# A grouped softmax on one ring of six tiles: the inner block and the clean-up taken out, the semaphores given to the context

## Chip, cores, metric

One NeuronCore of a Trainium2 chip. The metric is device time in microseconds (us). All runs told here were fast (none was clearly slower than the others of its kernel, and the granted clock was 1.0 in each). "Span" is the time from the first to the last instruction of a profiled run; the device time is 1.8 us longer than the span (1330.5 to 1328.7).

## What is computed

```python
B, N, D, G = 4, 4096, 4352, 8          # float32
x_g = x.reshape(B, N, G, D // G)       # groups of 544
e = np.exp(x_g - x_g.max(axis=-1, keepdims=True))
out = (e / e.sum(axis=-1, keepdims=True)).reshape(B, N, D)
```

16384 rows of 17 KB are read once and written once: 285.21 MB each way.

## The kernel before

A tile is 256 rows: 128 partitions of two rows (4.25 MB). Six tile buffers form a ring, and a tile is overwritten in place by its exponentials and then by its results. There are 64 tiles. Three engines work: SP (the sync engine) issues loads and stores, the vector engine (DVE) finds the maxima and scales, the scalar engine (ACT) takes exponentials and sums. DVE and ACT run a hardware loop of ten turns of twelve rows, and eight rows after it.

```python
    ctx.enter_context(tc.tile_critical(no_gpsimd_drain=True))
    ctx.enter_context(nc.cleanup_on_exit())              # clears the semaphores at the end, then a barrier
    bufs = [...]                                         # six tiles
    landed = [nc.alloc_semaphore(f"landed{b}") for b in range(NT)]
    stored = [nc.alloc_semaphore(f"stored{b}") for b in range(NT)]
    ...                                                  # max_done, exp_done, rec_done, scaled

    with nc.Block(no_gpsimd_drain=True) as block:        # ends in a barrier of all engines
        @block.sync
        def _(sync):
            def load(t):
                b = t % NT
                if t >= NT:
                    sync.wait_ge(stored[b], 16 * (t // NT))
                sync.dma_start(out=bufs[b][:, :], in_=xt[t]).then_inc(landed[b], 16)

            for t in range(NT - 1):
                load(t)
            for t in range(nt):
                sync.wait_ge(scaled, R * (t + 1))
                sync.dma_start(out=ot[t], in_=bufs[t % NT][:, :]).then_inc(stored[t % NT], 16)
                if t + NT - 1 < nt:
                    load(t + NT - 1)
            for b in range(NT):                          # the last wait for stores
                sync.wait_ge(stored[b], 16 * ((nt - b + NT - 1) // NT))

        @block.vector
        def _(vector):
            vector_max(0)
            with loop(vector):                           # nc.Fori, its head pinned to slot 0
                for s in range(S):
                    vector_max((s + 1) % S)
                    vector_scale(s)
            ...                                          # the last eight rows
        @block.scalar
        def _(scalar):
            ...                                          # the same with scalar_exp
```

Of the kernel before, what the change touches and what calls it, by code (L numbers as in the profile page):

```python
# [1 line left out]

# [5 lines left out]


@with_exitstack  # L10
def kernel(
    ctx: ExitStack,
    tc: tile.TileContext,
    x: bass.AP,
    out: bass.AP,
):
    nc = tc.nc
    G = 8
    P = 128
    R = 2  # L20
    NT = 6
    S = R * NT
    xf = x.flatten_outer_dims()
    of = out.flatten_outer_dims()
    N, D = xf.shape
    Dg = D // G
    nt = N // (P * R)
    nr = nt * R
    turns = (nr - 1) // S
    f32 = mybir.dt.float32  # L30
    X = mybir.AxisListType.X
    Exp = mybir.ActivationFunctionType.Exp
    xt = xf.rearrange("(t p r) d -> t p (r d)", p=P, r=R)
    ot = of.rearrange("(t p r) d -> t p (r d)", p=P, r=R)

    ctx.enter_context(tc.tile_critical(no_gpsimd_drain=True))  # L36
    ctx.enter_context(nc.cleanup_on_exit())
    bufs = [ctx.enter_context(nc.sbuf_tensor(f"xt{b}", [P, R * D], f32)) for b in range(NT)]
    mx = ctx.enter_context(nc.sbuf_tensor("mx", [P, S, G], f32))
    sm = ctx.enter_context(nc.sbuf_tensor("sm", [P, S, G], f32))  # L40
    rs = ctx.enter_context(nc.sbuf_tensor("rs", [P, S, G], f32))
    landed = [nc.alloc_semaphore(f"landed{b}") for b in range(NT)]
    stored = [nc.alloc_semaphore(f"stored{b}") for b in range(NT)]
    max_done = nc.alloc_semaphore("max_done")
    exp_done = nc.alloc_semaphore("exp_done")
    rec_done = nc.alloc_semaphore("rec_done")
    scaled = nc.alloc_semaphore("scaled")

    def row(s):
        b, r = divmod(s, R)  # L50
        return bufs[b][:, r * D:(r + 1) * D].rearrange("p (g d) -> p g d", g=G)

    def vector_max(s):
        if s % R == 0:
            nc.vector.sem_inc(landed[s // R], -16).wait_op(landed[s // R], 16, "sem-ge")  # L55
        nc.vector.reduce_max(out=mx[:, s, :], in_=row(s), axis=X, negate=True).then_inc(max_done, 1)  # L56

    def vector_scale(s):
        nc.vector.sem_inc(exp_done, -1).wait_op(exp_done, 1, "sem-ge")  # L59
        nc.vector.reciprocal(out=rs[:, s, :], in_=sm[:, s, :]).then_inc(rec_done, 1)  # L60
        nc.vector.sem_inc(rec_done, -1).wait_op(rec_done, 1, "sem-ge")  # L61
        xr = row(s)
        for g in range(G):
            i = nc.vector.tensor_scalar_mul(  # L64
                out=xr[:, g, :], in0=xr[:, g, :], scalar1=rs[:, s, g:g + 1])
        i.then_inc(scaled, 1)

    def scalar_exp(s):
        nc.scalar.sem_inc(max_done, -1).wait_op(max_done, 1, "sem-ge")  # L69
        xr = row(s)  # L70
        for g in range(G):
            i = nc.scalar.activation(  # L72
                out=xr[:, g, :],
                in_=xr[:, g, :],
                func=Exp,
                bias=mx[:, s, g:g + 1],
                scale=1.0,
                accum_out=sm[:, s, g:g + 1],
            )
        i.then_inc(exp_done, 1)  # L80

    def loop(engine):

        return nc.Fori(
            0, turns, engines=OrderedEngineSet([engine.engine]), head_slot={engine.engine: 0})

    with nc.Block(no_gpsimd_drain=True) as block:  # L87


        @block.sync  # L90
        def _(sync):
            def load(t):
                b = t % NT
                if t >= NT:
                    sync.wait_ge(stored[b], 16 * (t // NT))
                sync.dma_start(out=bufs[b][:, :], in_=xt[t]).then_inc(landed[b], 16)

            for t in range(NT - 1):
                load(t)
            for t in range(nt):  # L100
                sync.wait_ge(scaled, R * (t + 1))
                sync.dma_start(out=ot[t], in_=bufs[t % NT][:, :]).then_inc(stored[t % NT], 16)
                if t + NT - 1 < nt:
                    load(t + NT - 1)
            for b in range(NT):
                sync.wait_ge(stored[b], 16 * ((nt - b + NT - 1) // NT))


        @block.vector
        def _(vector):  # L110
            vector_max(0)
            with loop(vector):
                for s in range(S):
                    vector_max((s + 1) % S)
                    vector_scale(s)
            for n in range(turns * S, nr):
                if n + 1 < nr:
                    vector_max((n + 1) % S)
                vector_scale(n % S)

        @block.scalar
        def _(scalar):
            scalar.preload_act_table(Exp)  # L123
            with loop(scalar):
                for s in range(S):
                    scalar_exp(s)
            for n in range(turns * S, nr):
                scalar_exp(n % S)


# [1 line left out]
_INS = ['x']  # L132
_OUTS = [((4, 4096, 4352), 'float32')]


# [23 lines left out]
```

## Time and profile before

| | before |
|---|---|
| device time, median of 3 runs | 1330.23 us (1329.97 to 1331.25) |
| share of the data queue in what 16 DMA engines have | 99.6% |
| DVE busy, ACT busy | 1041.5 us (78%), 764.4 us (58%) |
| steady beat, from load to load | 20.57 us per tile |
| from the end of the last wait for stores to the end of the span | 2.3 us |

The lines that carry this stand in the prediction. Read them in this order: is an engine full (no); is the data queue full (yes); does SP wait for arithmetic or for stores (for stores); how long is the beat.

### The profile page before, as it was taken

To read this page: it belongs to the slowest core of one execution; us is meant where nothing else is said; L and a number is where in the kernel's file an instruction comes from. 1 tells how busy PE (TensorE), PEld (TensorE's weight loads), DVE (VectorE), ACT (ScalarE), POOL (GpSimd) and SP (SyncE) were. 2 spreads that over 40 slices of the span, in tenths; PEclk is the share of its full clock that TensorE was granted. 3 is DMA by queue.
4 is the path that set the end of the run, shared out by engine and by line. 5 is a ranking of instruction groups with operands and counts; after the bars stand their busy time and mean duration, and the time that the engine had idled before them with its cause. 6 is when DMAs were issued, how large, how long until landed. Compare 5 with 4: busy or idle time off the path is not lost. (4 is left out here: it accounts for less than half of the span.)

```text
span 1328.7 us, 4036 instructions
## 1 busy us (share of the span) xinstructions
DVE 1041.5 (78%) x1280; ACT 764.4 (58%) x2049; POOL 0.2 (0%) x4
## 2 busy tenths in 40 slices
DVE  5999987787877878778778787787877877878770
ACT  3777765655656556555565565655655556556560
POOL 0000000000000000000000000000000000000000
DMA  9999999999999999999999999999999999999997
GB/s 401 418 434 434 434 430 428 432 436 433 435 433 431 429 436 434 436 435 430 429 436 434 435 435 432 428 435 435 434 436 434 429 431 436 434 435 434 431 430 336
DMA packets 18441, 570.51 MB, mean 429 GB/s; under 512 B 2048, under 2 KB 2048, under 8 KB 2048
## 3 DMA queue, kind: packets, MB, share of 16 engines
q1 hardware_dynamic: 18432, 570.43, 99.6%
q14 instruction: 9, 0.07, 0.0%
HBM read 285.21 MB, written 285.21 MB: 429 GB/s over the span
## 5 line engine op out<-in xcount | busy, mean ns | idle before, releaser
L72 ACT ACTIVATE xt<-xt,mx 128x544 f32<-128x544 f32 x1024 | 751.3, 735 | 528.7 <-ACTq L69 528.7
L56 DVE TENSOR_REDUCE mx<-xt 128x8 f32<-128x4352 f32 x128 | 599.1, 4680 | 234.0 <-DVEq L55 233.1
L64 DVE TENSOR_SCALAR xt<-xt,rs 128x544 f32<-128x544 f32 x1024 | 434.0, 497 | 19.2 <-DVEq L61 0.9
L72 ACT ACTIVATION_READ_ACCUMULATOR xt<-xt,mx 128x1 f32 x1024 | 191.1, 187 | 0.0
L60 DVE RECIPROCAL rs<-sm 128x8 f32<-128x8 f32 x128 | 24.5, 191 | 3.2 <-DVEq L59 3.2
L123 ACT ACT_TABLE_LOAD x1 | 1.3, 1283 | 0.9 <-SPq L36 0.9
L143 POOL MEMSET const-bfloat16-1.0<- 128x1 bf16 x1 | 0.1, 102 | 0.0
L143 POOL MEMSET const-uint8-127<- 128x1 uint8 x1 | 0.1, 102 | 0.0
L143 POOL MEMSET const-float32-0.0<- 128x1 f32 x1 | 0.1, 99 | 0.2 <-issue 0.2
L143 POOL MEMSET const-float32-1.0<- 128x1 f32 x1 | 0.1, 99 | 0.0
## 6 DMA issues: line engine op xcount, KB each, us to landing
xt<-in_x_dram SPq DMA_DIRECT2D x64, 4352.0 KB, 30.8
out_dram<-xt SPq DMA_DIRECT2D x64, 4352.0 KB, 40.7
```

Source lines behind the costliest of these rows:

```text
L56: nc.vector.reduce_max(out=mx[:, s, :], in_=row(s), axis=X, negate=True).then_inc(max_done, 1)
L60: nc.vector.reciprocal(out=rs[:, s, :], in_=sm[:, s, :]).then_inc(rec_done, 1)
L64: i = nc.vector.tensor_scalar_mul(out=xr[:, g, :], in0=xr[:, g, :], scalar1=rs[:, s, g:g + 1])
L72: i = nc.scalar.activation(out=xr[:, g, :], in_=xr[:, g, :], func=Exp, bias=mx[:, s, g:g + 1], scale=1.0, accum_out=sm[:, s, g:g + 1],)
L123: scalar.preload_act_table(Exp)
L143: nc = _bacc.Bacc("TRN2", target_bir_lowering=False, num_devices=1)
```

## The change

The intent is a plainer program: no inner block with a body per engine, and semaphores that the surrounding context owns and clears once, when it closes. Tiles, ring, loops, waits and arithmetic are as they were.

```diff
+    landed = [tc.alloc_semaphore(f"landed{b}") for b in range(NT)]
+    stored = [tc.alloc_semaphore(f"stored{b}") for b in range(NT)]
+    ...
     ctx.enter_context(tc.tile_critical(no_gpsimd_drain=True))
-    ctx.enter_context(nc.cleanup_on_exit())
     bufs = [...]
-    landed = [nc.alloc_semaphore(f"landed{b}") for b in range(NT)]
-    ...
-    with nc.Block(no_gpsimd_drain=True) as block:
-        @block.sync
-        def _(sync):
-            ...
-        @block.vector
-        def _(vector):
-            ...
+    for t in range(NT - 1):
+        load(t)
+    for t in range(nt):
+        store(t)
+        if t + NT - 1 < nt:
+            load(t + NT - 1)
+    for b in range(NT):
+        nc.sync.wait_ge(stored[b], 16 * ((nt - b + NT - 1) // NT))
+
+    nc.scalar.preload_act_table(Exp)
+    with loop(nc.scalar):
+        ...
+    vector_max(0)
+    with loop(nc.vector):
+        ...
```

More of the change, by code (lines that the diff above doesn't have):

```diff
@@ L34 @@
     ot = of.rearrange("(t p r) d -> t p (r d)", p=P, r=R)
+    landed = [tc.alloc_semaphore(f"landed{b}") for b in range(NT)]
+    stored = [tc.alloc_semaphore(f"stored{b}") for b in range(NT)]
+    max_done = tc.alloc_semaphore("max_done")
+    exp_done = tc.alloc_semaphore("exp_done")
+    rec_done = tc.alloc_semaphore("rec_done")
+    scaled = tc.alloc_semaphore("scaled")
     ctx.enter_context(tc.tile_critical(no_gpsimd_drain=True))
-    ctx.enter_context(nc.cleanup_on_exit())
     bufs = [ctx.enter_context(nc.sbuf_tensor(f"xt{b}", [P, R * D], f32)) for b in range(NT)]
@@ L41, with loop @@
     rs = ctx.enter_context(nc.sbuf_tensor("rs", [P, S, G], f32))
-    landed = [nc.alloc_semaphore(f"landed{b}") for b in range(NT)]
-    stored = [nc.alloc_semaphore(f"stored{b}") for b in range(NT)]
-    max_done = nc.alloc_semaphore("max_done")
-    exp_done = nc.alloc_semaphore("exp_done")
-    rec_done = nc.alloc_semaphore("rec_done")
-    scaled = nc.alloc_semaphore("scaled")
+    def loop(engine):
+        return nc.Fori(
+            0, turns, engines=OrderedEngineSet([engine.engine]), head_slot={engine.engine: 0})
     def row(s):
@@ L80, in scalar_exp @@
         i.then_inc(exp_done, 1)
-    def loop(engine):
-        return nc.Fori(
-            0, turns, engines=OrderedEngineSet([engine.engine]), head_slot={engine.engine: 0})
-    with nc.Block(no_gpsimd_drain=True) as block:
-        @block.sync
-        def _(sync):
-            def load(t):
-                b = t % NT
-                if t >= NT:
-                    sync.wait_ge(stored[b], 16 * (t // NT))
-                sync.dma_start(out=bufs[b][:, :], in_=xt[t]).then_inc(landed[b], 16)
-            for t in range(NT - 1):
-                load(t)
-            for t in range(nt):
-                sync.wait_ge(scaled, R * (t + 1))
-                sync.dma_start(out=ot[t], in_=bufs[t % NT][:, :]).then_inc(stored[t % NT], 16)
-                if t + NT - 1 < nt:
-                    load(t + NT - 1)
-            for b in range(NT):
-                sync.wait_ge(stored[b], 16 * ((nt - b + NT - 1) // NT))
-        @block.vector
-        def _(vector):
-            vector_max(0)
-            with loop(vector):
-                for s in range(S):
-                    vector_max((s + 1) % S)
-                    vector_scale(s)
-            for n in range(turns * S, nr):
-                if n + 1 < nr:
-                    vector_max((n + 1) % S)
-                vector_scale(n % S)
-        @block.scalar
-        def _(scalar):
-            scalar.preload_act_table(Exp)
-            with loop(scalar):
-                for s in range(S):
-                    scalar_exp(s)
-            for n in range(turns * S, nr):
-                scalar_exp(n % S)
@@ new lines, in load, with store @@
+    def load(t):
+        b = t % NT
+        if t >= NT:
+            nc.sync.wait_ge(stored[b], 16 * (t // NT))
+        nc.sync.dma_start(out=bufs[b][:, :], in_=xt[t]).then_inc(landed[b], 16)
+    def store(t):
+        nc.sync.wait_ge(scaled, R * (t + 1))
+        nc.sync.dma_start(out=ot[t], in_=bufs[t % NT][:, :]).then_inc(stored[t % NT], 16)
+    for t in range(NT - 1):
[4 more added lines that the diff above has]
+            load(t + NT - 1)
@@ new lines @@
+    for b in range(NT):
+        nc.sync.wait_ge(stored[b], 16 * ((nt - b + NT - 1) // NT))
+    nc.scalar.preload_act_table(Exp)
+    with loop(nc.scalar):
+        for s in range(S):
+            scalar_exp(s)
+    for n in range(turns * S, nr):
+        scalar_exp(n % S)
+    vector_max(0)
+    with loop(nc.vector):
+        for s in range(S):
+            vector_max((s + 1) % S)
+            vector_scale(s)
+    for n in range(turns * S, nr):
+        if n + 1 < nr:
+            vector_max((n + 1) % S)
+        vector_scale(n % S)
```

## The prediction

The sum came to -1.0 us: -0.5 for the block's exit, -0.5 for the clean-up, +0.1 for the larger clear, -0.1 at the front. The 0.005 for "faster by over 2%": what the trace before shows is that 64 beats of 20.57 us make 1316.5 us, more than the 1303.6 us needed. Rival B: its time of 1329 to 1330 is a guess of mine. So are the 1 to 2 us of rival D. The steps of the block's exit that the trace shows are a branch of SP (38 ns, at 1326.5 us), drains of ACT, DVE and SP, and semaphore steps of all five engines, the last at 1326.7 to 1326.9 us.

> **What bounds the kernel now.** I read the page's busy table and queue table first, then the stretches of the span, the waits of the sync queue, the issues in order of time, and last the instructions of the source lines that the change touches. The first question is whether any engine or only the transfers fill the span:
>
> ```profile
> DVE 1041.5 (78%) x1280; ACT 764.4 (58%) x2049; POOL 0.2 (0%) x4
> DMA  9999999999999999999999999999999999999997
> DMA packets 18441, 570.51 MB, mean 429 GB/s; under 512 B 2048, under 2 KB 2048, under 8 KB 2048
> q1 hardware_dynamic: 18432, 570.43, 99.6%
> q14 instruction: 9, 0.07, 0.0%
> ```
>
> No compute engine is full: the vector engine works 78% of the span. The data queue has packets under way for 99.6% of what 16 DMA engines have in 1328.7 us. All bytes are necessary (285.21 MB in, 285.21 MB out), so the transfers set the time. By stretches (columns: the stretch, its length, busy time and instructions of DVE, ACT, POOL, clock, DMA share, GB/s) the middle is flat:
>
> ```profile
> 35.00:300.00 265.00, 234.16 (x288) 171.92 (x462) 0.00 (x0) 1.00 1.00 431
> 600.00:900.00 300.00, 239.69 (x299) 175.67 (x471) 0.00 (x0) 1.00 1.00 434
> 1290.00:1329.00 39.00, 5.14 (x13) 3.99 (x12) 0.00 (x0) 1.00 0.80 345
> ```
>
> Only the last 39 us fall off (345 GB/s), and there compute has almost ended. Who waits for whom confirms it. The sync queue waits for transfers, not for arithmetic:
>
> ```profile
> SPq L96 <- DMA out_dram<-xt: 1141.2, 58, 20.7
> SPq L102 <- DVE xt L64: 102.4, 6, 33.3
> SPq L106 <- DMA out_dram<-xt: 28.0, 1, 28.0
> ```
>
> 1141.2 of 1328.7 us are spent before a load, until an old store has landed and freed its buffer. The issues in order of time show the beat:
>
> ```profile
> 1223.44 0.33 SPq L96 DMA_DIRECT2D xt<-in_x_dram  x1
> 1223.81 0.43 SPq L102 DMA_DIRECT2D out_dram<-xt  x1
> 1244.03 0.33 SPq L96 DMA_DIRECT2D xt<-in_x_dram  x1
> ```
>
> A load every 20.59 us. The same view has a load at 956.07 us and the one at 1244.03 us fourteen tiles later, so (1244.03 - 956.07) / 14 = 20.57 us per tile. One tile is 2 x 4352 KB = 8.913 MB, hence 433 GB/s. Per tile the vector engine needs 1041.5 / 64 = 16.3 us and the scalar engine 764.4 / 64 = 11.9 us, so even the vector engine has 4.3 us of slack per tile. 64 x 20.57 = 1316.5 us; the other 12.2 us are start, end and fixed instructions.
>
> [...] only 9 instruction packets (0.07 MB) in the whole span, too few for one reload in each of 10 turns.
>
> **The change part by part.** The title words (six tiles, 256 rows, hardware loops) describe both kernels. The diff leaves tile size, ring depth, order of loads and stores, every wait count, every vector and scalar instruction and both loops as they are. Three things change.
>
> (1) The inner block goes. On entry it costs at most a jump per engine. On exit each engine branches, drains and meets the others.
>
> (2) The clean-up on exit goes: a clear of a range of semaphores on POOL and one more barrier of all engines.
>
> (3) The semaphores are now the context's, cleared when it closes. The old trace already has a clear there, so this becomes a larger or a second clear in the same place.
>
> The cost is read from the instructions of each source line (L106 the last wait for stores, L87 the block, _compat.py:109 the clean-up, L154 the context):
>
> ```profile
> L106 SPq EVENT_SEMAPHORE  x3: 17/28/28, 1326.3 to 1326.4; - x3
> L87 SPq COMPARE_BRANCH  x1: 38/38/38, 1326.5 to 1326.5; - x1
> L87 PEldq EVENT_SEMAPHORE  x2: 51/51/51, 1.1 to 1326.9; - x2
> _compat.py:109 POOLq DRAIN  x2: 34/58/83, 1326.9 to 1327.1; - x2
> _compat.py:109 POOLq EVENT_SEMAPHORE_RANGE_CLEAR  x1: 117/117/117, 1327.0 to 1327.0; - x1
> _compat.py:109 PEldq EVENT_SEMAPHORE  x1: 51/51/51, 1327.4 to 1327.4; - x1
> L154 POOLq EVENT_SEMAPHORE_RANGE_CLEAR  x1: 67/67/67, 1328.4 to 1328.4; - x1
> ```
>
> (The two times after the durations are the first and the last start.) The last wait ends at 1326.4, the block's exit runs from 1326.5 to 1326.9, the clean-up from 1326.9 to 1327.4; then the critical section's exit (to 1327.7) and the context's two barriers (to 1328.7) remain. This is a serial chain after the last byte, so all of it lies on the path: 0.5 us for the block's exit and 0.5 us for the clean-up, together 1.0 us. Added: the larger clear. The old clean-up's clear took 117 ns, the context's 67 ns; if it becomes a second instruction, 0.1 us comes back. At the front, the first load starts at 0.95 us and the branches of all engines at 0.8 us (33 ns on SP); if the entry jump goes, the load starts up to 0.1 us earlier, and every transfer with it. Sum: -0.5 - 0.5 + 0.1 - 0.1 = -1.0 us. Between the two ends nothing moves. 1330.23 - 1.0 = 1329.2 us.
>
> **The rivals.**
>
> A: the context needs something the diff does not show, such as a clear or a barrier ahead of the critical section, because its semaphores are taken outside it. A round of barrier plus clear measures 0.5 us (the clean-up), so one such round at the front makes -0.5 us, 1329.7; two cancel the gain, 1330.2. Against it: nothing in the kernel asks for it.
>
> B: the loops are laid out otherwise without blocks of their own, [...] so each turn reloads. [...] Against it: the head is pinned in both kernels. Even then the vector engine has 6 x 4.3 = 26 us of slack per turn of six tiles (an estimate from the two rates above), so a stall of some us per turn vanishes under the transfers[...]. Time: 1329 to 1330.
>
> C: the first tiles run otherwise and the DMA queue runs dry at the start. The first store is issued at 37.5 us; the fifth load, issued by 3.7 us, needs 54.5 us to land, so it lands at about 58. The queue has some 20 us of work in hand; a few tenths cannot empty it. No change.
>
> D: the ragged end moves. The last store is issued at 1297.9 and waited for 28.0 us. The DMA share falls to 0.54 in 1318 to 1322, 0.28 in 1322 to 1324 and 0.08 in 1324 to 1326: some of the 16 engines finish us before the others. Which one is last may differ by 1 to 2 us[...]. That has no direction, and is the main cause of the width of my range.
>
> E: the vector engine becomes the bound. It would need over 4.3 us more per tile; no instruction is added to it. I give it nothing.
>
> **Range and chances.** The three runs before lie in 1329.97 to 1331.25, so chance alone is about +-0.6 us. The sum has an error of about 0.5 us (A, the clears), the ragged end about 1 us. I predict 1329.2 us, 1327.9 to 1330.8 in 8 of 10. 2% is 26.6 us. Faster by over 2% would need 1303.6 us[...]: 0.005, for an error in my reading. Slower by over 2% needs a stall of 26 us that reaches the transfers, which the slack in B and C absorbs: 0.01. Within 2%: 0.985.
>
> **What would show each step right or wrong.** Right: same busy times of DVE and ACT within 1 us, the same packets and MB, loads still 20.57 us apart, the last wait for stores ending near 1326.4, then only about 1.3 us to the end of the span where there were 2.3, no lines of the block and no clean-up clear, and a somewhat longer or second clear at L154's successor. Rival A shows as barriers ahead of the first load, which then starts after 1.2 us instead of 0.95. B shows as over 20 instruction packets and gaps on DVE and ACT once per turn. D shows as a last landing that has moved by more than 1 us with an unchanged chain behind it. The prediction is wrong if the load interval leaves 20.57 us in the middle of the span, or if the instructions behind the last landing take 2 us or more.

## The result

The first comparison had four runs of each kernel: 1330.57 us after (1330.07 to 1331.24) and 1330.49 us before (1329.97 to 1331.25). The ratio is 1.0, with a 95% interval of 0.9983 to 1.0018. (A ratio here is the mean time of one kernel's fast runs over that of the other's of the same rounds, so not quite the ratio of the medians quoted.) The time lies in the predicted range, but the microsecond that I had expected to gain is not to be seen in it.

The page of the changed kernel, the same parts as before:

```profile
DVE 1041.5 (78%) x1280; ACT 764.4 (57%) x2049; POOL 0.2 (0%) x4
...
q1 hardware_dynamic: 18432, 570.43, 99.5%
q14 instruction: 8, 0.07, 0.0%
```

Busy times and data packets are the same. The packed traces have eight instruction packets of 8 KB at much the same moments in both kernels (at 2, 7, 18, 24, 80, 110, 755 and 1243 us before), so the loops do not fetch their code anew in each of their ten turns. The ninth packet of before starts 0.1 us before the end of its span; it comes up again below. The waits of the sync queue (engine, line, waited for: us in total, times, longest):

```profile
SPq L92 <- DMA out_dram<-xt: 1141.8, 58, 21.3
SPq L96 <- DVE xt L69: 102.0, 6, 33.3
SPq L105 <- DMA out_dram<-xt: 28.0, 1, 28.0
```

These are the three waits of before to 0.6 us. Then the closing instructions by source line (L105 is the last wait for stores, L43 the critical section, L149 the context; the last two times are the first and the last start):

```profile
L105 SPq EVENT_SEMAPHORE  x3: 17/28/28, 1328.0 to 1328.1; - x3
...
L43 SPq NOP  x2: 13/13/13, 0.7 to 1328.6; - x2
...
L149 POOLq EVENT_SEMAPHORE_RANGE_CLEAR  x1: 139/139/139, 1329.0 to 1329.0; - x1
```

The block's exit and the clean-up are gone. From the end of the last wait to the end of the last instruction the changed kernel takes 1.28 us, the kernel before 2.29 us: 1.0 us less, the forecast. (These closing times, here and below, are read from the starts and durations in the packed traces, which are kept to the nanosecond; the span that `prof` prints is rounded to 0.1 us.) But the last wait ends 1.7 us later, at 1328.15 instead of 1326.42. Where does that come from? The issues of the sync queue in order of time, before:

```profile
89.19 0.33 SPq L96 DMA_DIRECT2D xt<-in_x_dram  x1
...
109.76 0.33 SPq L96 DMA_DIRECT2D xt<-in_x_dram  x1
...
131.30 0.33 SPq L96 DMA_DIRECT2D xt<-in_x_dram  x1
```

and after:

```profile
89.22 0.33 SPq L92 DMA_DIRECT2D xt<-in_x_dram  x1
...
111.30 0.33 SPq L92 DMA_DIRECT2D xt<-in_x_dram  x1
...
131.84 0.33 SPq L92 DMA_DIRECT2D xt<-in_x_dram  x1
...
1245.77 0.33 SPq L92 DMA_DIRECT2D xt<-in_x_dram  x1
```

At 89 us the two traces are level. The next beat takes 20.57 us before and 22.08 us after, but the one after that 21.54 and 20.54, so at 131 us the changed kernel is only 0.5 us behind. The rest gathers in small steps: 1.5 us at 421 us, 1.6 at 545, 1.7 from 771 us on. The last load is issued at 1244.03 before and 1245.77 after, and in both the last wait ends 82.4 us after it. So the 1.7 us were lost in many beats, most of them in the first third of the run, and not at the end. Either the change makes those beats worse, or they scatter from run to run whatever the kernel. The experiments decide this.

### The profile page after: what moved, and what is told of

Read it like the earlier page. It is cut to its first block, busy times and chain, and to the rows that moved or that the text cites. A ratio compares the mean times of both kernels' runs of the same rounds, so it can differ in the third digit from the quotient of the medians.

```text
span 1329.4 us, 4004 instructions
## 1 busy us (share of the span) xinstructions
DVE 1041.5 (78%) x1280; ACT 764.4 (57%) x2049; POOL 0.2 (0%) x4
## 3 DMA queue, kind: packets, MB, share of 16 engines
q1 hardware_dynamic: 18432, 570.43, 99.5%
## 5 line engine op out<-in xcount | busy, mean ns | idle before, releaser
L77 ACT ACTIVATE xt<-xt,mx 128x544 f32<-128x544 f32 x1024 | 751.2, 734 | 530.4 <-ACTq L74 530.4
```

What stands on the lines that cost most here:

```text
L77: i = nc.scalar.activation(out=xr[:, g, :], in_=xr[:, g, :], func=Exp, bias=mx[:, s, g:g + 1], scale=1.0, accum_out=sm[:, s, g:g + 1],)
```

## The experiments

Theory T1: the change is worth about 1 us in every run, all of it behind the last byte, and the early beats scatter by more than that in both kernels. Rival T2: without the block the transfers themselves run worse and eat the gain. Kernels of one call share the runs of the kernel before on their chip.

### The changed kernel again, and the kernel before as a control

No edit in either; five rounds.

> The changed kernel once more. Theory T1 (the removed closing steps are worth about 1.2 us in every run, and the moment at which the last store lands scatters by 1 to 2 us from run to run, whatever the kernel): the profile shows 1.0 to 1.2 us from the end of the last wait for stores to the end of the span, the last wait ends anywhere in 1325.5 to 1328.5 us, and the median over the rounds is 0.3 to 1.5 us below the kernel before. Rival T2 (without the block the transfers themselves run worse by about 1 to 2 us and eat the gain): the last wait again ends at 1328 us or later, and the two medians are equal within 0.3 us.

> The kernel before, unchanged, as a control. Both theories: a ratio of 1.000 within 0.001. T1: its last wait for stores need not end at 1326.4 us again, it may be off by 1 us or more, and 2.3 us follow it. T2: the last wait ends within 0.5 us of 1326.4.

The last waits, first of the changed kernel again, then of the control:

```profile
L105 SPq EVENT_SEMAPHORE  x3: 17/28/28, 1326.5 to 1326.6; - x3
```

```profile
L106 SPq EVENT_SEMAPHORE  x3: 17/28/28, 1326.5 to 1326.7; - x3
```

The changed kernel's last wait ends at 1326.6 this time, 1.5 us earlier than in its first profile and level with the control's 1326.7. T2 asked for 1328 or later. From there to the end it is 1.28 us in the changed kernel and 2.29 us in the control, as in the first two profiles; for the changed kernel I had expected 1.0 to 1.2, having read the first profile's wait too late. The medians are 1329.84 us (1329.26 to 1329.93) for the changed kernel, 1330.76 us for the control and 1331.42 us for the shared nine runs of before. That is 0.9 us under the control and 1.6 us under the nine, the latter just more than the 1.5 I had allowed. The ratio, 0.9988 (0.9975 to 1.0002), still includes 1. On the control, T1 and T2 differed only in whether its last wait may move: it moved by 0.3 us, which decides nothing.

### Transfers without arithmetic

```diff
     def vector_max(s):
         if s % R == 0:
             nc.vector.sem_inc(landed[s // R], -16).wait_op(landed[s // R], 16, "sem-ge")
-        nc.vector.reduce_max(...)
     def vector_scale(s):
-        ...                        # wait, reciprocal, eight scalings; and all of scalar_exp
+        nc.vector.sem_inc(scaled, 1)
```

> The changed kernel with all arithmetic taken out: the vector engine only waits for a landed tile and counts it as scaled, so loads and stores go on alone (wrong result on purpose). If the transfers set the time, as the prediction says: 1318 to 1332 us, loads 20.5 to 20.7 us apart in the middle. If arithmetic is part of the beat: below 1304 us (faster by over 2%).

Measured: 1330.67 us (1330.09 to 1331.19; result wrong), ratio 0.9994 (0.9979 to 1.0009). Two loads from the middle:

```profile
566.63 0.33 SPq L69 DMA_DIRECT2D xt<-in_x_dram  x1
...
587.22 0.33 SPq L69 DMA_DIRECT2D xt<-in_x_dram  x1
```

Without one maximum, exponential or product the kernel takes as long. The transfers set the time. It also shows the early scatter: its first 18 steady beats (from the seventh load on) together were 4.1 us longer than 18 x 20.57 us, and its last load went out at 1245.71 us, as late as in the first profile of the changed kernel. So neither arithmetic nor its order against the transfers is needed for late beats.

### More work for the vector engine

```diff
+        nc.vector.reduce_max(out=spare[:, s, :], in_=row(s)[:, 0:3, :], axis=X)
         nc.vector.reduce_max(out=mx[:, s, :], in_=row(s), axis=X, negate=True).then_inc(max_done, 1)
```

> The changed kernel with one more reduction over three of eight groups per row (about 1.8 us each, an estimate from 4.68 us for eight groups, so 3.5 us per tile and 227 us in all), results unused. The vector engine then needs 19.8 of 20.57 us per tile. If its slack is off the path, as the prediction says: the time stays within 3 us of the kernel before, the loads still 20.5 to 20.7 us apart. If the vector engine takes part in setting the beat: slower by 20 us or more.

```profile
DVE 1262.3 (95%) x1408; ACT 764.6 (58%) x2049; POOL 0.2 (0%) x4
```

Measured: 1330.62 us (1330.12 to 1332.18), ratio 0.9997 (0.9982 to 1.0012). 220.8 us of added vector work cost nothing: DVE is at 95% and the beat is still 20.57 us. Of the slack of 4.3 us per tile that the prediction leaned on, 220.8 / 64 = 3.45 us were used here without a cost.

### The three steps of the change on twelve tiles

```diff
-    nt = N // (P * R)
+    nt = 12
```

With 12 of 64 tiles there is less run for scatter (less only in part: the uneven beats lie in the first twenty tiles). The middle kernel keeps the block, and takes the semaphores from the context without a clean-up.

> The kernel before on 12 of 64 tiles only (wrong result on purpose: the rest of the output is not written), so that less can scatter between start and end. About 12 x 20.57 + 12 = 259 us. Its closing steps after the last wait should be the 2.3 us of the full kernel.

> The short kernel with the block kept and the clean-up taken out (semaphores of the context): one half of the change. T1: 0.4 to 0.7 us below the short kernel before, and closing steps of 1.6 to 1.9 us. T2 says nothing of this one.

> The changed kernel on 12 of 64 tiles. T1: 1.0 to 1.3 us below the short kernel before, closing steps of 1.0 to 1.2 us, first load at the same 0.95 us. T2: no more than 0.5 us below it, because the transfers end later.

The last waits and the clears of the three, each in its own fence, in this order:

```profile
L106 SPq EVENT_SEMAPHORE  x3: 17/28/28, 236.8 to 257.3; - x3
...
L154 POOLq EVENT_SEMAPHORE_RANGE_CLEAR  x1: 67/67/67, 259.0 to 259.0; - x1
```

```profile
L106 SPq EVENT_SEMAPHORE  x3: 17/27/28, 236.0 to 256.5; - x3
...
L154 POOLq EVENT_SEMAPHORE_RANGE_CLEAR  x1: 157/157/157, 257.7 to 257.7; - x1
```

```profile
L105 SPq EVENT_SEMAPHORE  x3: 17/28/28, 236.4 to 256.9; - x3
...
L149 POOLq EVENT_SEMAPHORE_RANGE_CLEAR  x1: 139/139/139, 257.8 to 257.8; - x1
```

| short kernel | median us | range | last wait to end of span |
|---|---|---|---|
| before | 260.30 | 259.93 to 261.11 | 2.02 |
| block kept, no clean-up | 259.88 | 259.76 to 259.96 | 1.63 |
| changed | 259.35 | 258.98 to 259.98 | 1.27 |

The time falls by 0.42 us with the clean-up and by 0.53 us with the block, 0.95 us together (0.99 by the means). That is slightly less than the 1.0 to 1.3 I had expected, and more than the 0.5 that T2 allowed. But four runs of one kernel spread by up to 1.2 us, and the profiled run of the middle kernel (259.96 us) was no longer than that of the changed one (259.98), so the times do not show the split. The closing steps do: they fall by 0.39 us with the clean-up and by 0.36 us with the block, 0.75 us together. The 1.27 us of the changed kernel lie above the 1.0 to 1.2 I had expected. The fourth combination, clean-up without block, was left out, because in the code nothing would order its clear behind the transfers' increments. The clear of the context grows from 67 to 139 or 157 ns once it takes over the sixteen semaphores.

The short kernel before closes in 2.02 us, and not in the 2.3 of the full one, which I had not expected. The difference is one drain of the vector engine at the closing of the context. The line of the full kernel before, then that of the short one:

```profile
L154 DVEq DRAIN  x2: 10/69/128, 1327.9 to 1328.3; - x2
```

```profile
L154 DVEq DRAIN  x2: 10/10/10, 258.4 to 259.0; - x2
```

In the full kernel before, one of the two drains took 128 ns and started only at 1327.9 us, when ACT, PE and SP had done theirs between 1327.5 and 1327.8. It held up the barrier, whose semaphore steps start at 1328.2 us. The control has it too (130 ns), the changed kernel never (10 ns each in its three profiles). The packed traces show what it goes with: in both, an instruction packet of 8 KB starts 0.67 us after the start of the late drain (at 1328.61 and 1328.87 us). This is the ninth packet of before. The short kernels have no such packet at the end, and in the full changed kernel the next one starts over 1 us after the end of the span. A third late drain, of 144 ns, lies among the twenty blocks at the end below, and a packet follows it after 0.67 us too. So the late drain goes together with an instruction packet that happens to fall into the closing of the kernel before. That the packet is code of the vector engine and holds up its drain is my guess: the trace does not say which engine a packet is for, and no experiment moved it.

### Twenty empty blocks, behind and in front

```diff
+    for _ in range(20):
+        with nc.Block(no_gpsimd_drain=True):
+            pass
```

> The changed kernel with twenty empty blocks behind the last wait for stores. If an empty block at the end lies wholly on the path at the 0.4 to 0.5 us that the old trace shows for the block's exit: 8 to 11 us slower than the changed kernel. If what was seen in the old trace overlapped with waiting anyway: under 3 us.

> The changed kernel with twenty empty blocks ahead of the first load. If the front is as serial as the end: the first load starts about 0.48 us x 20 = 9.6 us later than 0.95 us (0.48 us each is what the twenty at the end gave), and the whole kernel is 8 to 11 us slower; the 20 us of queued work behind the first loads cannot hide what comes before the first byte. If the start is hidden by something: under 3 us.

With the blocks behind the last wait: 1338.99 us (1338.46 to 1339.31), 8.1 us over the kernel before of the same rounds (1330.90), so about 9.1 us over the changed kernel if its gain of 1.0 is counted. The blocks' instructions show the length:

```profile
L126 SPq DRAIN  x20: 7/7/7, 1326.4 to 1335.3; - x20
```

From the first to the twentieth drain 8.9 us pass, so a block costs 8.9 / 19 = 0.47 us on the mean. Most of the 19 steps take 0.44 us; two take 0.86 and 0.72 us, the longer one with the late vector drain. With the blocks in front: 1339.47 us (1339.28 to 1340.03), 9.4 us over the changed kernel of the same rounds (1330.05). Its first load:

```profile
9.79 3.23 SPq L92 DMA_DIRECT2D xt<-in_x_dram  x5
```

The first load starts at 9.79 instead of 0.95 us: 8.84 / 20 = 0.44 us per block. Both ends of this kernel, which is bound by its transfers, are bare: nothing hides a barrier before the first byte or behind the last one. An empty block added costs 0.44 us at either end; taking out the real one gave 0.36 us.

### The loop heads elsewhere

```diff
-            0, turns, engines=..., head_slot={engine.engine: 0})
+            0, turns, engines=..., head_slot={engine.engine: 100})
```

> The changed kernel with the heads of both loops pinned to slot 100 instead of 0[...]. Prediction's rival B: the instruction packets grow from 8 or 9 to 20 or more if reloading happens in each turn, the scalar engine shows a gap once per turn, and the time stays within 2 us all the same, since the vector engine has about 26 us of slack per turn. Against it: slower by 10 us or more.

```profile
q14 instruction: 6, 0.05, 0.0%
```

Measured: 1330.55 us (1330.25 to 1330.62), ratio 0.9996 (0.998 to 1.0011). The packets fell to 6, and ACT's idle time is 529.8 us, as in the other kernels (528.7 before, 530.4 after). The experiment did not bring about the reload that it was to test, so it says only that a shifted loop costs nothing measurable here. That a loop head at slot 100 would bring reloads was an assumption of mine; no run of this case shows it. What a reload in each turn would cost remains untried.

### One transfer per row: an attempt to be faster

```diff
-        nc.sync.dma_start(out=bufs[b][:, :], in_=xt[t]).then_inc(landed[b], 16)
+        for r in range(R):
+            nc.sync.dma_start(out=bufs[b][:, r * D:(r + 1) * D],
+                              in_=xt[t][:, r * D:(r + 1) * D]).then_inc(landed[b * R + r], 16)
```

(and the stores likewise, each as soon as its row is scaled)

> The changed kernel with each load and each store cut in two, one per row of a partition, each row stored as soon as it is scaled: an attempt to beat both kernels. If the last microseconds are lost because a tile is large: 3 to 6 us faster. If, as I believe, the rate of the transfers sets the time and the beginning and end only a little: within 2 us of the changed kernel.

Measured: 1337.84 us (1337.62 to 1337.97), 0.5% slower; both of my expectations were wrong (7.8 us over the changed kernel of the same rounds). The page's queue (packets, MB, share):

```profile
q1 hardware_dynamic: 36864, 570.44, 99.7%
```

Two loads from the middle, in order of time:

```profile
567.87 0.81 SPq L92 DMA_DIRECT2D xt<-in_x_dram  x2
...
588.53 0.81 SPq L92 DMA_DIRECT2D xt<-in_x_dram  x2
```

Twice the packets carry the same bytes, and the beat is 20.66 us instead of 20.57. Over 64 tiles that makes 5.8 us, most of the loss. Per engine and tile there are 18432 / 16 / 64 = 18 packets more for 0.09 us: 5 ns each, an estimate that puts all of it down to the packets. The first store goes out at 23.92 us instead of about 37.5 and nothing is won by it, since the queue was full anyway.

### The changed kernel a third time

> The changed kernel a third time, on the chip of these runs. T1 as refined by the runs so far: 0.7 to 1.5 us below the kernel before of the same rounds, 1.1 to 1.3 us from the end of the last wait to the end of the span, and the last wait ends 82 to 83 us after the last load is issued, wherever that is. T2 (the gain is eaten in the transfers): equal to the kernel before within 0.3 us.

Measured: 1330.05 us (1329.17 to 1330.42) beside 1331.10 us (1329.93 to 1331.99, nine runs) of the kernel before: 1.05 us less, ratio 0.9992 (0.9978 to 1.0005). The last load went out at 1244.54 us, and the last wait ended 82.4 us later:

```profile
L105 SPq EVENT_SEMAPHORE  x3: 17/28/28, 1326.8 to 1326.9; - x3
```

Again 1.28 us followed. All of it is as T1 expected. T2 had asked for equal times within 0.3 us, and for a last wait at 1328 us or later in e1.

Over the three comparisons that hold the unedited changed kernel there are 14 runs of it with a mean of 1330.06 us, and 27 of the kernel before with 1331.05 us. From the scatter of the runs (standard deviations 0.55 and 0.70) the difference of 1.0 us has a standard error of 0.2 us. That is rather too small: by comparison the differences of the means are +0.06, -1.46 and -1.12 us, further apart than the scatter within them explains, and each ratio taken alone has an interval that includes 1. So the total favours T1 and speaks against a loss in the transfers as large as the gain, but it does not give the gain's size. A loss of a few tenths is not excluded either: the first 18 steady beats were 3.0 us longer than 18 x 20.57 in both full profiles with the block, and 1.9 to 4.4 us in the eight without. The size rests on the closing steps, which were 2.29 us in both full profiles of before and 1.28 us in all three of the changed kernel. No full-length kernel tried was faster than the changed one.

## Why the prediction was right, and where its steps were off

**The bound.** Right, and now shown: transfers alone take 1330.67 us, and 221 us more vector work take nothing.

**The closing steps.** The sum was right (1.0 us predicted, 2.29 to 1.28 us measured), in part by luck: two terms were too large, and a gain that was not predicted made up for them. The clean-up was read rightly: the prediction nets -0.5 and +0.1, and taking it out of the short kernel gave 0.39 us, the larger clear included. The block was not: 0.5 us predicted, 0.36 us measured. I had counted to its exit a branch of the sync engine right behind the last wait, with 0.16 us from its start to the next step. The changed kernel still has this branch:

```profile
L92 SPq COMPARE_BRANCH  x1: 38/38/38, 1328.2 to 1328.2; - x1
```

The rest of the full kernel's gain, 2.29 against 2.02 us, is the late vector drain that I had not counted.

**The added clear.** Predicted +0.1 us; measured 139 - 67 = 72 ns for the instruction itself.

**The front.** Predicted -0.1 us; measured nothing: the first load starts at 0.94 or 0.95 us in all profiles of both kernels. I had taken the branches at 0.8 us for the block's entry. They belong to the context (L154 before), and the changed kernel has that of the sync engine at the same moment:

```profile
L149 SPq COMPARE_BRANCH  x1: 33/33/33, 0.8 to 0.8; - x1
```

This term of the sum was wrong, but too small to matter.

**The rivals.** A (something added at the front) did not occur. B (reloads of the loops) did not occur: 8 or 9 packets in all, none of them once per turn. C did not occur. D had the right size and the wrong place. I put the scatter down to the ragged end, but the last wait ended 82.4 us after the last load in both first profiles, in both later profiles of the changed kernel and in the control (82.3 to 83.2 us in the edited full kernels with this ring). What moves is mostly the beat of the first twenty tiles: in the ten full profiles with this ring the first 18 steady beats (from the seventh load on) were together 1.9 to 4.4 us longer than 18 x 20.57, and between the two first profiles the last load moved by 1.7 us. Single beats there take 20.5 to 22.1 us, later ones 20.57 us but for a few (20.65 us in the last ten beats of both kernels with twenty blocks). It happens with and without arithmetic. What in the transfers causes it stays open.

**The range.** 1327.9 to 1330.8 held the first median. But I took the scatter of three runs, +-0.6 us, for that of the kernel. Later runs of the kernel before lie from 1329.93 to 1332.50 us with a mean of 1331.05, so the 1330.23 that I started from was low, and 1329.2 with it: the 14 runs of the changed kernel have a mean of 1330.06 us. With such a scatter a gain of 1 us need not show in four runs of each.

## What to carry to other kernels

In this kernel, whose queue is full from end to end, only steps before the first byte and behind the last one were found to take out, and there every empty block added counted in full: about 0.45 us, which is 0.03% of this kernel and would be more of a short one. Measure such a gain where it arises, from the last landing to the end of the span, because the scatter of the transfers buries it in the total, and on the shortened kernel it was still as large as the gain. To read the cost of a step off a trace, check that its instructions are really gone in the other kernel: two branches here were not. Before you make something smaller to start earlier, check whether the queue was waiting for it at all.
